# The MLP's first token block, made during the last chunk's convolution

## The chip, the core and the metric

One core of a Trainium2 chip runs the whole kernel. The metric is the device time of one execution in microseconds (us). TensorE (PE) does the matmuls, with the loading of its weights shown as PEld; VectorE (DVE), ScalarE (ACT) and GpSimd (POOL) work on elements; SyncE (SP) mainly issues DMA transfers. Each engine takes its instructions in the order of the compiled program, and waits where an operand or a buffer isn't there yet.

## The reference

One decoder layer on x of 2048 rows by 1024 columns, float32:

```python
h = rms_norm(x, attn_norm_g); z = h @ w_in          # q, k, v, gate_b, gate_c, xc
y_attn = swa_sink_attention(norm(q), norm(k), v, sinks)   # window 128, 8 heads of 64
y_conv = gate_b * short_conv(gate_c * xc, conv_w)         # 3 taps, 512 channels
x = x + concat(rms_norm(y_attn), rms_norm(y_conv)) @ w_out
x = x + square(relu(rms_norm(x) @ w_up)) @ w_down         # 4096 wide
```

## The kernel before, in words

**Mixer.** The rows are done in four chunks of 512 (`NCHUNK`, `NT` = 4 tiles of 128 rows each; the attention's tiles are called b0 to b15, so the last chunk has b12 to b15). Each fp32 matrix is split into a high and a low part, and a product is three matmuls (`mm3`, lines 267 to 269). For a tile, `qk_transpose` turns queries and keys (PE: L619, L621; ACT and DVE split them: L624, L625, L628, L629), `softmax` multiplies them (`psc`, L646) and works on the scores on ACT and DVE (L654 to L671), and `values` turns the probabilities (`ptp`, L682), splits and masks them (L688 on ACT, L689 on DVE, L695 on POOL), multiplies by v (`po`, L734) and finishes the tile on ACT and DVE (L742 to L750). The convolution of a chunk has two `conv_pair`s. Each has three groups of weights (wc, wx, wb), two output tiles for each group, 24 matmuls for a tile (`pc`, `px`, `pb`); DVE multiplies and adds the taps (L798 to L803, L815, L819). The output projection of a chunk has a half for the convolution (half 1, `pout3_1_*` in the last chunk) and one for the attention (half 0). Half 0 is left over to the next chunk, where it runs as `before`, ahead of the convolution.

**Order of the work.** `besides` is a generator with everything that runs beside the attention: `before`, then the two conv_pairs, then the projection's half 1. The attention's functions call `fill(n)` to step it, with the numbers of the table FILL. On top of that stands a scheduler: each instruction has a priority (`ahead(i)` raises it by `PRIO[chunk][i]`, which for `ahead(9)` in the last chunk is 0), and the scheduler decides each engine's order when the program is compiled. SP's transfers are one queue, in order. Weights come from DRAM by `weights` (L236, 1 MB each for the high and the low part) into two pairs of buffers of tag "w" and one of tag "raw", in turn: in the last chunk wc and wx in "w", wb in "raw", for both pairs, then the four pieces of the projection (`w_wo`).

**First block of the MLP.** The MLP multiplies 2x2 blocks by seven products instead of eight (`ORDER`). Its first token block is rows 0 to 1023, done by chunks 0 and 1. Each x operand is made from x1 in DRAM: `load_turned` (L308) loads four pieces of 128 KB for a quarter jj, `turned` transposes (L314) and scales (L315) on DVE, `x_put` (L319) stores it in `xop`, and `x_sums` (L325) makes the four differences. For each of the four jj there are blocks 1 and 2 (turned from the first 512 rows, `xm0`), block 3 and one unnamed (from the second 512 rows, `xm1`), and the sums 5, 6, 7 and 4.

`prepare_firsts` (L890) makes blocks 1 and 2 for all jj during the last chunk's convolution, a step at every seventh step of it (`FIRST_X`). `prepare_mlp` (L908) does the rest beside the projection's half 1, in the buffers of the tags "h0" and "h1"; it reads blocks 1 and 2 back from `xop`. Behind it come the residual's rows for chunk 3 (`x1_3`, L950, tag "x1", 4 buffers of 1024 columns) in the code's order ahead of the projection, and the loads of the last weights. The chunk before stores its rows by L880.

Of the kernel before, what the change touches and what calls it, by code (L numbers as in the profile page):

```python
# [7 lines left out]
F32 = mybir.dt.float32  # L8
# [4 lines left out]
ALU = mybir.AluOpType  # L13
# [3 lines left out]
P = 128  # L17
# [17 lines left out]
CH = 512  # L35
NT = CH // P
NCHUNK = S // CH
# [7 lines left out]
ORDER = (1, 2, 6, 5, 3, 7, 4)  # L45
# [4 lines left out]
BW = 512  # L50
NB = BW // P
# [18 lines left out]
CHP = CH + 32  # L70
STEPS = 3
TS = 32
FIRST_X = 7
REST = 7
LATER = 250

# [27 lines left out]
def hymba_layer(  # L104
# [19 lines left out]
    nc = tc.nc  # L124
# [11 lines left out]
    pool = mixers_ctx.enter_context(tc.tile_pool(name="work", bufs=1))  # L136
# [4 lines left out]
    x1_dram = dram.tile([S, D], F32, name="x1_dram")  # L141
# [3 lines left out]
    xop_dram = [  # L145
        [dram.tile([P, BLK], F32, name=f"xop{tb}_{i}") for i in range(len(ORDER))] for tb in range(NTB)
    ]
# [7 lines left out]
    def bank(tag, name):  # L155
        return psum.tile([P, 512], F32, tag=tag, name=name, bufs=BANKS[tag])

    def row(tag, name, bufs, dt=F32):

        return pool.tile([P, D], dt, tag=tag, name=name, bufs=bufs)  # L160
# [28 lines left out]
    def rsqrt(dst, ms):  # L189

        nc.gpsimd.tensor_scalar(ms, ms, EPS, None, op0=ALU.add)
        nc.gpsimd.tensor_tensor(dst, ms, mhalf[:, : ms.shape[1]], op=ALU.pow)
# [3 lines left out]
    def ahead(i):  # L196

        offset = PRIO[stage[0]][i]
        return tc.high_priority(offset=offset) if offset else nullcontext()
# [103 lines left out]
    def load_turned(xb, src, r0, jj):  # L303

        for pg in range(4):
            rows = src[r0 : r0 + BW].rearrange("(q i) (k c) -> i k q c", i=TS, k=2)
            c0 = jj * P + pg * TS
            nc.sync.dma_start(  # L308
                xb[pg * TS : (pg + 1) * TS].rearrange("p (k q c) -> p k q c", k=2, c=TS), rows[:, :, :, c0 : c0 + TS]
            )  # L310

    def turned(xb, k, dst, g, rs_row):

        nc.vector.transpose(dst, xb[:, k * BW : (k + 1) * BW])  # L314
        nc.vector.scalar_tensor_tensor(dst, dst, g, rs_row, op0=ALU.mult, op1=ALU.mult)  # L315

    def x_put(tb, jj, i, b):

        nc.sync.dma_start(xop_dram[tb][ORDER.index(i)][:, jj * BW : (jj + 1) * BW], b)  # L319

    def x_sums(tb, jj, b11, b21, b12, b22, t1):


        def sub(i, dst, a, b):
            nc.vector.tensor_tensor(dst, a, b, op=ALU.subtract)  # L325
            x_put(tb, jj, i, dst)

        x_put(tb, jj, 3, b22)
        sub(5, t1, b12, b11)
        sub(6, b11, b22, t1)  # L330
        sub(7, b12, b22, b12)
        sub(4, b21, b21, b11)
# [12 lines left out]
    def parts(pool_, tag, name):  # L345
        return [pool_.tile([P, KD, CH], F32R, tag=f"{tag}{s}", name=f"{tag}{s}_{name}", bufs=1) for s in range(2)]

    def prepare(src, r0, gb, dst, name):

        xs = []  # L350

        def fetch(t):
            xt = row("xt", f"xt_{name}_{t}", 2)
            nc.sync.dma_start(xt, src[r0 + t * P : r0 + (t + 1) * P, :])
            with ahead(8):
                norm(xt, gb, f"{name}_{t}")
                xs.append(xt)

        fetch(0)
        fetch(1)  # L360
        yield
        for t in range(NT):
            yield from transposed(xs[t], dst, t, f"{name}_{t}")
            if t + 2 < NT:
                fetch(t + 2)
# [55 lines left out]
    h = parts(pool, "h", "a0")  # L421
# [103 lines left out]
    with tc.tile_pool(name="mix_small", bufs=1) as mix_small, tc.tile_pool(name="mix", bufs=1) as mix:  # L525
# [359 lines left out]
                                    rs_out(c)  # L885
                    yield

        rows_x = []

        def prepare_firsts():  # L890

            rows = pool.tile([P, 2, BW], F32, tag="gb", name="rs_rows", bufs=1)
            rows_x.append(rows)
            for i in range(2):
                nc.sync.dma_start(rows[:, i], rs_dram[i].partition_broadcast(P))
            for jj in range(NB):
                xb = row("xt", f"xt_m0_{jj}", 2)
                load_turned(xb, x1_dram, 0, jj)
                yield
                bs = row("xt", f"xm0_{jj}", 2)  # L900
                for k in range(2):
                    b = bs[:, k * BW : (k + 1) * BW]
                    with ahead(9):
                        turned(xb, k, b, g_cols[:, NB * k + jj : NB * k + jj + 1], rows[:, 0])
                    x_put(0, jj, 1 + k, b)
                    yield

        def prepare_mlp():  # L908

            xs = [pool.tile([P, 8, CH], F32, tag=f"h{i}", name=f"xm{i}", bufs=1) for i in range(2)]  # L910
            rows = rows_x[0]
            xts = {}

            def fetch(jj):
                for k in range(2):
                    src = xop_dram[0][ORDER.index(1 + k)]
                    nc.sync.dma_start(xs[0][:, 2 * jj + k], src[:, jj * BW : (jj + 1) * BW])
                xts[jj] = row("xt", f"xt_m1_{jj}", 2)
                load_turned(xts[jj], x1_dram, BW, jj)

            fetch(0)
            fetch(1)
            yield
            for jj in range(NB):
                bs = [xs[0][:, 2 * jj + k] for k in range(2)] + [xs[1][:, 4 * (jj % 2) + k] for k in range(3)]
                with ahead(9):
                    for k in range(2):
                        turned(xts[jj], k, bs[2 + k], g_cols[:, NB * k + jj : NB * k + jj + 1], rows[:, 1])
                if jj + 2 < NB:
                    fetch(jj + 2)  # L930
                x_sums(0, jj, *bs)
                yield

        def besides(c, before, h, yt, rc, x1, h_next, z_next):

            yield from before
            ssc = mix.tile([P, CH], F32, tag="ssc", name=f"ssc{c}", bufs=1)
            firsts_x = prepare_firsts() if c + 1 == NCHUNK else iter(())
            for j in range(2):
                for i, _ in enumerate(conv_pair(c, h, j, yt, ssc)):  # L940
                    if i % FIRST_X == 0:
                        next(firsts_x, None)
                    yield
            for _ in firsts_x:
                pass
            x1 += [] if c else x0
            for t in range(NT if c else 0):
                r = (c * NT + t) * P
                xr = row("x1", f"x1_{c}_{t}", NT)
                nc.sync.dma_start(xr, xf[r : r + P, :])  # L950
                x1.append(xr)
            out = out_projection(c, 1, yt, rc, x1)
            if c + 1 < NCHUNK:
                h_next += parts(pool, "h", f"h{c + 1}")
                steps = prepare(xf, (c + 1) * CH, g_row[0], h_next, f"a{c + 1}")
            else:
                steps = prepare_mlp()
            for i, _ in enumerate(steps):
                yield
                for j in range(STEPS):  # L960
                    next(out, None)
                    yield
                    if (i, j) == PC:
                        pc = bank("tr", f"pc{c}")
                        for t in range(NT):
                            nc.tensor.matmul(
                                pc[:, t : t + 1], ssc[:, t * P : (t + 1) * P], mean, start=True, stop=True
                            )
                        ms = mix_small.tile([P, NT], F32, tag="msc", name=f"ms_c{c}", bufs=1)

                        with tc.high_priority(offset=SOON):
                            if c:
                                nc.vector.tensor_copy(ms, pc[:, :NT])
                                rsqrt(rc, ms)
                            else:
# [97 lines left out]
        g_cols = const.tile([P, KD], F32, name="g_cols")  # L1073
# [15 lines left out]
        for c in range(NCHUNK):  # L1089
            left, h, z = mixers(c, left, h, z)  # L1090
# [8 lines left out]
    pool = up_ctx.enter_context(tc.tile_pool(name="mlp_up", bufs=1, reuse_waits="tile"))  # L1099
# [247 lines left out]
    steps = [(p, g) for p in ORDER_DOWN for g in range(NCG // 2)]  # L1347
# [93 lines left out]
    pool = ctx.enter_context(tc.tile_pool(name="mlp_down", bufs=1, reuse_waits="tile"))  # L1441
# [131 lines left out]
```

## Time and profile before

| what | value |
|---|---|
| time, median of 3 runs | 1964.53 us (1963.91 to 1967.26) |
| the profiled execution | 1962.7 us |
| its span in the trace | 1961.0 us |
| mean granted clock of TensorE | 0.989 |
| PE busy | 1915.9 us (98%) |
| DVE, ACT, POOL busy | 1213.3, 827.3, 275.2 us |
| the attention's last left projection ends, the last chunk's convolution begins | 564 us |
| the projection's half 1 waits longest | 674.4 to 693.2 us |
| the MLP's first matmuls | about 730 us |

The page cuts the span into 40 slices of 49 us and gives the busy tenths of each engine in each. A table by stretch (the windows) gives the length of the stretch, then busy us and instruction counts of PE, PEld, DVE, ACT and POOL, the granted clock of TensorE (1.00 is full), the share of the DMA engines and GB/s. A group's row has: line, engine, operation, output and inputs, shape, count, then busy us and the mean of one in ns, then idle time before it and what ended it. A row of the waits has the engine and its line, who released it, us in total, how often, the longest.

### The profile page before, as it was taken

Reading aid. Unit: us, or ns where it says so; the run is one execution under the profiler, and the core shown is the slowest. Engines: PE = TensorE matmul, PEld = TensorE weight load, DVE = VectorE, ACT = ScalarE, POOL = GpSimd, SP = SyncE. Lnnn points to the kernel's source line nnn. Section 1 sums busy time; section 2 is a strip of 40 time slices with the busy share of each in tenths; the row PEclk is TensorE's granted clock in tenths of the full one; section 3 lists DMA queues with packets and bytes.
Section 4 is the critical chain, followed back from the end, with each engine's and each line's share of the span. In section 5 each row is a group of like instructions: output and inputs, shape, how many; then the busy total and the mean of one; then the engine's idle time right before and its main releaser. Section 6 shows DMA issues by size and latency. Waiting matters only on the chain.

```text
span 1961.0 us, 24748 instructions
## 1 busy us (share of the span) xinstructions
PE 1915.9 (98%) x8961; PEld 1595.4 (81%) x8961; DVE 1213.3 (62%) x1896; ACT 827.3 (42%) x1577; POOL 275.2 (14%) x475
## 2 busy tenths in 40 slices
PE   9999999999999689899999999999999999999999
PEld 9878877888888468788888888888888888888887
DVE  4885657447567838788878766666544334447541
ACT  6564444335344217355466555454332232222320
POOL 2122212312222201222201101011000000100000
PEclk9999999999999789999999999999999999999999
DMA  9774865574675778978775544437964457776641
GB/s 323 279 278 122 264 251 172 197 233 151 211 238 179 209 278 284 221 216 235 242 227 207 172 150 163 140 122 275 385 235 139 151 169 227 249 233 215 217 140 54
DMA packets 270540, 414.37 MB, mean 211 GB/s; under 512 B 85064, under 2 KB 174160, under 8 KB 258640
## 3 DMA queue, kind: packets, MB, share of 16 engines
q1 hardware_dynamic: 241664, 337.25, 52.7%
q0 software_dynamic: 15488, 51.40, 7.2%
q10 hardware_dynamic: 13264, 24.13, 3.3%
q8 instruction: 71, 1.16, 0.3%
q14 instruction: 53, 0.43, 0.1%
HBM read 286.87 MB, written 125.84 MB: 210 GB/s over the span
## 4 chain that ended last, share of the span: by engine, by line
PE 91%; DMA 3%; DVE 3%; ACT 1%; POOL 1%; issue 0%; SPq 0%; DVEq 0%; ACTq 0%
PE d L1533 31%; PE u L1426 30%; PE pout L268 3%; PE pout L267 3%; PE pout L269 3%; PE pz L267 2%; PE pz L268 2%; PE pz L269 2%; PE pc_c L269 2%; PE px_c L267 1%; PE px_c L269 1%; PE px_c L268 1%; PE pc_c L267 1%; PE pc_c L268 1%; PE psc_b L646 1%; PE po_b L734 1%
## 5 line engine op out<-in xcount | busy, mean ns | idle before, releaser
L1426 PE MATMUL u<-op_x,wop 128*128 128x512 f32 x2688 | 612.5, 390 | 5.4 <-DVE wop L398 5.4
L1533 PE MATMUL d<-op_w,op_f 128*128 128x512 f32 x2688 | 609.4, 389 | 0.0
L1426 PEld LDWEIGHTS u<-op_x,wop 128*128 128x128 f32 x2688 | 506.3, 188 | 111.5 <-DVE wop L398 5.8
L1533 PEld LDWEIGHTS d<-op_w,op_f 128*128 128x128 f32 x2688 | 504.7, 188 | 104.6
L382 DVE TENSOR_TENSOR op_f<-op_f 128x1024 fp32r<-128x1024 f32 x112 | 136.9, 1224 | 234.2 <-ACT op_f L381 233.9
L381 ACT CAST op_f<-op_f 128x1024 fp32r<-128x1024 f32 x112 | 117.6, 1051 | 355.2 <-DMA op_f<-fop 354.7
L397 ACT CAST wop<-wu 128x512 fp32r<-128x512 f32 x156 | 96.4, 620 | 92.4 <-PE u L1426 89.9
L398 DVE TENSOR_TENSOR wop<-wu,wop 128x512 fp32r<-128x512 f32 x156 | 110.1, 707 | 36.1 <-ACT wop L397 18.3
L1162 POOL DMA_DIRECT2D fop<-s x96 | 52.1, 543 | 447.9 <-DVE s L1165 443.5
L1168 DVE TENSOR_TENSOR u<-u,u 128x512 f32<-128x512 f32 x128 | 87.7, 685 | 22.9 <-PE u L1426 22.9
L382 DVE TENSOR_TENSOR op_w<-raw,op_w 128x1024 fp32r<-128x1024 f32 x56 | 68.3, 1221 | 25.0 <-ACT op_w L381 24.8
L381 ACT CAST op_w<-raw 128x1024 fp32r<-128x1024 f32 x56 | 58.8, 1052 | 43.2 <-PE d L1533 20.4
L267 PE MATMUL pout<-w_wo,yt_c 128*128 128x512 f32 x128 | 52.6, 417 | 18.8 <-DMA w_wo<-wo 18.8
L663 ACT ACTIVATE sc_b<-sc_b,ngm_b 128x128 f32<-128x128 f32 x128 | 49.6, 389 | 30.9 <-DVE ngm_b L660 30.9
L1174 ACT ACTIVATE u<-u 128x512 f32<-128x512 f32 x64 | 40.4, 632 | 47.7 <-DVE u L1168 45.7
L695 POOL TENSOR_SCALAR_AFFINE_SELECT pp_b<-pp_b 128x512 fp32r<-128x512 f32 x60 | 42.3, 715 | 117.0 <-ACT pp_b L688 59.0
L1375 POOL DMA_DIRECT2D wds<-raw x16 | 8.5, 534 | 332.5 <-DVE raw L1373 322.8
L381 ACT CAST op_x<-op_x 128x1024 fp32r<-128x1024 f32 x28 | 29.1, 1049 | 59.3 <-DMA op_x<-xop 59.0
L397 ACT CAST wop<-wu_s 128x512 fp32r<-128x512 f32 x64 | 39.4, 619 | 33.6 <-PE u L1426 29.6
L398 DVE TENSOR_TENSOR wop<-wu_s,wop 128x512 fp32r<-128x512 f32 x64 | 45.9, 718 | 11.6 <-ACT wop L397 11.4
L268 PE MATMUL pout<-w_wo,yt_c 128*128 128x512 f32 x128 | 51.8, 405 | 0.8 <-DMA w_wo<-wo 0.8
L269 PE MATMUL pout<-w_wo,yt_c 128*128 128x512 f32 x128 | 52.2, 408 | 0.0
(253 smaller groups left out, 3139.8 us busy)
## 6 DMA issues: line engine op xcount, KB each, us to landing
op_f<-fop SPq DMA_DIRECT2D x112, 512.0 KB, 4.3
raw<-in_w_down_dram SPq DMA_DIRECT2D x72, 512.0 KB, 4.3
wu<-in_w_up_dram SPq DMA_DIRECT2D x128, 256.0 KB, 3.9
w_wo<-wo SPq DMA_DIRECT2D x24, 1024.0 KB, 6.8
fop<-s POOLq DMA_DIRECT2D x96, 256.0 KB, 2.5
fop<-u ACTq DMA_DIRECT2D x64, 256.0 KB, 2.7
op_x<-xop SPq DMA_DIRECT2D x28, 512.0 KB, 7.4
w_q<-qkv SPq DMA_DIRECT2D x24, 512.0 KB, 6.0
```

Of the source, the lines that this page charges most:

```text
L267: nc.tensor.matmul(ps, st(0), mv(0), start=first, stop=False)
L268: nc.tensor.matmul(ps, st(0), mv(1), start=False, stop=False)
L269: nc.tensor.matmul(ps, st(1), mv(0), start=False, stop=last)
L381: nc.scalar.copy(op[:, 0], raw)
L382: nc.vector.tensor_tensor(op[:, 1], raw, op[:, 0].bitcast(F32), op=ALU.subtract)
L397: splits.append(nc.scalar.copy(hi, blk).ins)
L398: nc.vector.tensor_tensor(lo, blk, hi.bitcast(F32), op=ALU.subtract)
L663: nc.scalar.activation(sc[:, hd, :], sc[:, hd, :], AF.Exp, bias=ngm[:, hd : hd + 1], accum_out=den[:, hd : hd + 1])
L1162: eng.dma_start(fop_dram[tb][ORDER_DOWN.index(i)][n // 2][:, n % 2], b)
L1168: return nc.vector.tensor_tensor(dst, ps, b, op=ALU.add).ins
L1426: nc.tensor.matmul(pt, wops[i][:, a, k, :], xops[tb, p][k // 2][:, b, k % 2, :], start=p not in GOES_ON and k + j == 0, stop=k + j == NB + ...
L1533: nc.tensor.matmul(ps[tb][j], fs[tb][:, a, k, j * P : (j + 1) * P], w[:, b, k, :], start=first and p not in GOES_ON and k + n == 0, stop=l ...
```

## The change

`prepare_firsts` goes, and `prepare_mlp` does both parts. It starts in `before` (a step at every fourth, `FIRST_X`), and goes on in the conv_pairs (a step at every fourth, `SECOND_X`). The second half uses the rows of tag "xt" for the turned blocks and rows of tag "x1", the residual's, for the blocks read back and the sums. The puts are collected and issued a step later (`put_late`). What isn't done when the convolution ends is issued right there, ahead of the residual's rows. Beside the projection there are now eight empty steps where there were five with work. New lines of the changed kernel: the differences are L940, the turned loads are called at L924; lines behind the change have moved by about 22.

```diff
-FIRST_X = 7
+FIRST_X, SECOND_X = 4, 4
...
-        def prepare_firsts():
+        def prepare_mlp():
...
+            def put(jj, i, b):
+                late.append((jj, i, b))
+
+            def put_late():
+                for jj, i, b in late:
+                    x_put(0, jj, i, b)
+                late.clear()
+
+            def fetch(i, jj):
+                xb = row("xt", f"xt_m{i}_{jj}", 2)
+                load_turned(xb, x1_dram, i * BW, jj)
+                return xb
+
             for jj in range(NB):
-                xb = row("xt", f"xt_m0_{jj}", 2)
-                load_turned(xb, x1_dram, 0, jj)
+                xb = fetch(0, jj)
                 yield
-                bs = row("xt", f"xm0_{jj}", 2)
+                bs = halves(row("xt", f"xm0_{jj}", 2))
                 for k in range(2):
-                    b = bs[:, k * BW : (k + 1) * BW]
                     with ahead(9):
-                        turned(xb, k, b, g_cols[:, NB * k + jj : NB * k + jj + 1], rows[:, 0])
-                    x_put(0, jj, 1 + k, b)
-                    yield
-
-        def prepare_mlp():
-
-            xs = [pool.tile([P, 8, CH], F32, tag=f"h{i}", name=f"xm{i}", bufs=1) for i in range(2)]
...
+                        turned(xb, k, bs[k], gain(k, jj), rows[:, 0])
+                    put(jj, 1 + k, bs[k])
+                yield
+                put_late()
             for jj in range(NB):
-                bs = [xs[0][:, 2 * jj + k] for k in range(2)] + [xs[1][:, 4 * (jj % 2) + k] for k in range(3)]
+                xb = fetch(1, jj)
+                b11, b21 = halves(row("x1", f"xm1_{jj}", NT))
+                for i, b in ((1, b11), (2, b21)):
+                    nc.sync.dma_start(b, xop_dram[0][ORDER.index(i)][:, jj * BW : (jj + 1) * BW])
+                put_late()
+                yield
+                b12, b22 = halves(row("xt", f"xm0_{jj}", 2))
+                t5, t6 = halves(row("x1", f"xm2_{jj}", NT))
                 with ahead(9):
-                    for k in range(2):
-                        turned(xts[jj], k, bs[2 + k], g_cols[:, NB * k + jj : NB * k + jj + 1], rows[:, 1])
-                if jj + 2 < NB:
-                    fetch(jj + 2)
-                x_sums(0, jj, *bs)
+                    turned(xb, 0, b12, gain(0, jj), rows[:, 1])
+                put_late()
                 yield
+                with ahead(9):
+                    turned(xb, 1, b22, gain(1, jj), rows[:, 1])
+                put(jj, 3, b22)
+                yield
+
+                def sub(i, dst, a, b):
+                    with ahead(9):
+                        nc.vector.tensor_tensor(dst, a, b, op=ALU.subtract)
+                    put(jj, i, dst)
+
+                put_late()
+                sub(5, t5, b12, b11)
+                sub(6, t6, b22, t5)
+                yield
+                put_late()
+                sub(7, b12, b22, b12)
+                sub(4, b21, b21, t6)
+                yield
+            put_late()
...
-            yield from before
+            turning = prepare_mlp() if c + 1 == NCHUNK else iter(())
+            for i, _ in enumerate(before):
+                if i % FIRST_X == 0:
+                    next(turning, None)
+                yield
             ssc = mix.tile([P, CH], F32, tag="ssc", name=f"ssc{c}", bufs=1)
-            firsts_x = prepare_firsts() if c + 1 == NCHUNK else iter(())
             for j in range(2):
                 for i, _ in enumerate(conv_pair(c, h, j, yt, ssc)):
-                    if i % FIRST_X == 0:
-                        next(firsts_x, None)
+                    if i % SECOND_X == 0:
+                        next(turning, None)
                     yield
-            for _ in firsts_x:
+            for _ in turning:
                 pass
...
-                steps = prepare_mlp()
+                steps = range(2 * NT)
```

More of the change, by code (lines that the diff above doesn't have):

```diff
@@ L886, in out_projection @@
                     yield
-        rows_x = []
-        def prepare_firsts():
+        def prepare_mlp():
             rows = pool.tile([P, 2, BW], F32, tag="gb", name="rs_rows", bufs=1)
-            rows_x.append(rows)
             for i in range(2):
                 nc.sync.dma_start(rows[:, i], rs_dram[i].partition_broadcast(P))
+            halves = lambda xt: [xt[:, k * BW : (k + 1) * BW] for k in range(2)]
+            gain = lambda k, jj: g_cols[:, NB * k + jj : NB * k + jj + 1]
+            late = []
+            def put(jj, i, b):
[8 more added lines that the diff above has]
+                return xb
@@ L908, in prepare_mlp @@
-        def prepare_mlp():
-            xs = [pool.tile([P, 8, CH], F32, tag=f"h{i}", name=f"xm{i}", bufs=1) for i in range(2)]
-            rows = rows_x[0]
-            xts = {}
-            def fetch(jj):
-                for k in range(2):
[L916 to L923, printed above, removed]
-            for jj in range(NB):
-                bs = [xs[0][:, 2 * jj + k] for k in range(2)] + [xs[1][:, 4 * (jj % 2) + k] for k in range(3)]
-                with ahead(9):
-                    for k in range(2):
-                        turned(xts[jj], k, bs[2 + k], g_cols[:, NB * k + jj : NB * k + jj + 1], rows[:, 1])
-                if jj + 2 < NB:
-                    fetch(jj + 2)
-                x_sums(0, jj, *bs)
-                yield
```

## The prediction

> **What bounds the kernel now.** I read the page first. The span is 1961.0 us, and TensorE (PE) is busy for 98% of it, so only a stretch in which PE stands or runs at half clock can give time back, and a new such stretch costs its whole length.
>
> ```profile
> span 1961.0 us, 24748 instructions
> PE   9999999999999689899999999999999999999999
> ...
> PEclk9999999999999789999999999999999999999999
> ```
>
> Each slice is 49 us. The dips are in slices 14 and 15 (637 to 735 us): the end of the last chunk's convolution and its output projection, where the change works. Next I cut that place into stretches; the first column after the window is its length, then busy time of PE, weight loads, DVE, ACT and POOL, then the granted clock and the DMA share.
>
> ```profile
> 564.00:645.00 81.00, 81.00 (x403) 67.97 (x402) 56.93 (x130) 40.04 (x134) 12.76 (x24) 1.00 0.64 181
> 645.00:649.00 4.00, 2.19 (x13) 1.33 (x11) 4.00 (x8) 1.87 (x4) 1.74 (x3) 1.00 0.65 154
> 649.00:659.20 10.20, 7.02 (x24) 5.58 (x25) 7.88 (x15) 3.56 (x9) 5.83 (x7) 0.50 0.95 301
> 659.20:674.40 15.20, 14.13 (x60) 10.36 (x58) 12.38 (x24) 4.00 (x7) 2.53 (x5) 1.00 0.93 208
> 674.40:676.30 1.90, 0.01 (x1) 0.00 (x0) 1.86 (x4) 0.00 (x0) 0.79 (x2) 1.00 1.07 381
> 676.30:693.20 16.90, 0.00 (x0) 0.03 (x1) 9.54 (x15) 0.00 (x0) 0.00 (x0) 0.50 0.85 289
> 693.20:700.20 7.00, 6.21 (x14) 4.45 (x15) 0.00 (x0) 0.00 (x0) 0.00 (x0) 0.50 1.00 421
> ```
>
> The convolution up to 645 us has no hole at all: 81.00 of 81.00 us. From 645 to 700.2 us PE misses 1.81 + 3.18 + 1.07 + 1.89 + 16.90 + 0.79 = 25.6 us. The waits say for what, and the chain of waits says why that came late:
>
> ```profile
> PE pout L267 <- DMA w_wo<-wo: 18.8, 1, 18.8
> PE po_b L734 <- DVE pp_b L689: 4.9, 3, 2.8
> ```
> ```profile
> 684.19 1.91 DVE xm L325 x3
> 686.12 0.32 SPq L319
> 686.49 0.45 SPq L236
> 686.99 8.57 DMA w_wo<-wo
> ```
>
> The 18.8 us are one wait for the weights of the second half of the convolution's projection. Their load (L236) stands on SP's queue behind the x_put transfers (L319), and the last of these waits for DVE's sums (L325). The weights are late because SP is in order, not because DMA is short.
>
> **What the change removes.** Transposes, scalings, sums and puts all go ahead of the residual's row loads and of the projection's weights; in the compiled order of the changed kernel no put stands on SP before the projection's loads any more. So the 18.8 us go. What is late next is the weight load itself: its pair of buffers comes free at the convolution's last matmul, and the first projection half (48 matmuls and b15's value products, over 11 us) covers a landing of 8.57 us. I cost it at nothing; without the cover it is 8.57 us. The 4.9 us for pp_b leave this place too, but come back below, since the chains of b14 and b15 stay. Half clock goes with the holes: 7.02 and 6.21 us of work at clock 0.50 would take half, 3.5 and 3.1 us less. Removed: 25.6 + 6.6 = **32.2 us**.
>
> **What it adds.** The work itself is small: 8 transposes, 8 scalings and 16 sums of one block are pulled into the convolution, some 23 us of DVE by the rows below, where DVE is busy 56.93 of 81.00 us. That much would fit. What counts is the order. Before, the compiled order lays score, transpose and value products of the attention one by one between convolution matmuls; in the changed kernel they stand in bunches (16 psc_b12, 16 psc_b13, then 44 matmuls of pc_c without a break, then ptp_b12, po_b12, 16 psc_b14, ptp_b13, po_b13, then 44 of px_c, and so on). In a bunch PE has nothing else to run while ACT, DVE and POOL make its operands, and in DVE's order the new transposes and sums now stand ahead of just these operands. SP also has each low half of a weight pair behind stores, turned loads and puts. The durations (count, busy us, mean ns):
>
> ```profile
> L646 PE MATMUL psc_b<-kw,qt_b 128*128 128x256 f32 x64 | 16.4, 282 | 0.0
> L315 DVE SCALAR_TENSOR_TENSOR xm<-xm,g_cols,rs_rows 128x512 f32<-128x512 f32 x12 | 9.0, 757 | 0.1
> L314 DVE STREAM_TRANSPOSE xm<-xt_m 128x512 f32<-128x512 f32 x12 | 8.2, 698 | 0.4 <-PE pb_c L268 0.4
> L325 DVE TENSOR_TENSOR xm<-xm 128x512 f32<-128x512 f32 x12 | 7.6, 685 | 0.1
> L803 DVE SCALAR_TENSOR_TENSOR y_c<-u_c,cw,y_c 128x512 f32<-128x512 f32 x8 | 6.2, 779 | 0.1
> L743 DVE TENSOR_TENSOR o_b<-po_b,o_b 64x512 f32<-64x512 f32 x8 | 5.5, 684 | 0.4 <-ACT o_b L742 0.4
> L689 DVE TENSOR_TENSOR pp_b<-ptp_b,pp_b 128x512 fp32r<-128x512 f32 x8 | 5.3, 677 | 2.7 <-ACT pp_b L688 2.6
> L688 ACT CAST pp_b<-ptp_b 128x512 fp32r<-128x512 f32 x8 | 4.4, 588 | 8.5 <-PE ptp_b L682 8.5
> L625 DVE TENSOR_TENSOR qt_b<-ptq_b,qt_b 64x512 fp32r<-64x512 f32 x6 | 4.1, 688 | 1.8 <-ACT qt_b L624 1.7
> L325 DVE TENSOR_TENSOR xm<-xm,xm 128x512 f32<-128x512 f32 x4 | 3.2, 796 | 0.1
> L798 DVE TENSOR_TENSOR u_c<-px_c,u_c 128x512 f32<-128x512 f32 x4 | 2.7, 686 | 4.3 <-PE px_c L269 4.3
> L801 DVE TENSOR_SCALAR y_c<-u_c,cw 128x512 f32<-128x512 f32 x4 | 1.9, 486 | 0.5 <-POOL halo L799 0.5
> L747 DVE TENSOR_TENSOR at_b<-o_b,at_b 128x512 fp32r<-128x512 f32 x4 | 2.7, 684 | 0.0
> L629 DVE TENSOR_TENSOR kw<-ptk_b,kw 64x128 fp32r<-64x128 f32 x6 | 1.7, 289 | 0.1
> L628 DVE TENSOR_TENSOR kw<-ptk_b,kw 64x128 fp32r<-64x128 f32 x6 | 1.7, 282 | 1.3 <-ACT kw L627 1.2
> L749 DVE TENSOR_TENSOR o_b<-o_b 128x256 f32<-128x256 f32 x4 | 1.7, 421 | 0.8 <-ACT o_b L748 0.7
> L750 DVE TENSOR_TENSOR o_b<-o_b 128x128 f32<-128x128 f32 x4 | 1.1, 287 | 0.1
> ```
> ```profile
> w_wc<-wc SPq DMA_DIRECT2D x4, 1024.0 KB, 7.7
> ```
> ```profile
> 541.94 0.80 SPq L236 DMA_DIRECT2D w_wc<-wc  x2
> ...
> 565.01 0.32 SPq L880 DMA_DIRECT2D x_dram<-x  x1
> ```
>
> I lay the changed orders on a time axis with these rows; the stalls, in order:
> 1. *First weights.* Both halves of w_wc were issued at 541.94 us. The low half now stands behind the store of chunk 2's last rows (565.01), so it lands at about 565.4 + 7.7 = 573. PE's work ahead of its first use (32 psc_b of some 0.12 us each when they follow one another, a few others) lasts from 564.0 to about 569.5; the bunch psc_b13 also waits for DVE's qt_b13 behind a transpose. 3 to 6 us, I take 4.3.
> 2. *After pc_c.* psc_b14 needs the second half of qt_b14. On DVE stand ahead of it: two L689, one L625, b14's keys (L628, L629) and a small copy of values, together about 1 us, two L314, two L315, and then L625 itself: 1.35 + 0.69 + 1 + 1.40 + 1.51 + 0.69 = 6.6, and about 2.6 us for the first transpose, cast and hand-overs: 9.2. PE has 3.2 us of po_b12 and transposes beside it: 6.0. Then ptp_b13 to po_b13 is the kind of chain that cost 1.8 and 3.2 us above (645 to 659): 2.3. Together 8.3, between 3 (if the first L625s run early) and 10.5.
> 3. *After px_c.* psc_b15 needs the second half of qt_b15. After the last px_c matmul DVE has L798 0.69, L801 0.49, two L803 1.56, two L743 1.37, first L625 and L747 1.37, b15's keys (L628, L629) and b12's squares (L749, L750) 0.28 + 0.29 + 0.42 + 0.29 = 1.28, two L314 1.40, two L315 1.51, four sums (three at 0.685, one at 0.796) 2.85, and L625 0.69: 13.2 us. PE has 1.4 us of transposes and pb_c beside it: 11.8, between 8 and 14. This is the largest term, and no other matmul may pass it.
> 4. *After pb_c*, the rest of psc_b15, then ptp_b14 and po_b14: the chain of item 2's end twice, 4.6, between 2 and 7.
> 5. *Later weights* behind the puts of the third and fourth block: 1.5, between 0 and 4.
>
> Idle time added: 4.3 + 8.3 + 11.8 + 4.6 + 1.5 = 30.5 us, between 16 and 41.5. The clock comes on top. In the rows above the granted clock went to 0.50 at 649.0 after the 1.81 us of holes from 645 on. A later stall shows what the return costs:
>
> ```profile
> 804.00:809.40 5.40, 5.40 (x13) 4.24 (x14) 5.39 (x10) 2.67 (x6) 1.62 (x3) 0.50 1.06 324
> 809.40:820.00 10.60, 10.60 (x48) 8.76 (x48) 10.56 (x18) 4.80 (x9) 0.54 (x1) 1.00 0.92 268
> ```
>
> 13 matmuls at 0.415 us instead of 0.221 are 2.5 us; the stretch from 649 cost 3.5. With one drop for each of items 1 to 4 at 2.7 that is 11 us, between 2.5 (item 3 alone) and 17.5 (one more, at 3.5 each).
>
> The Trainium skill speaks of this ("TensorE: Matmul & The Clock Gate", "HAM oscillation — how this bites in real kernels"): the clock falls when PE idles for more than some 3.4 us at a stretch. The row of 645 to 649, where the clock fell after less idle than that, does not bear it out literally. By the page items 1 and 4, which come in pieces, would keep the clock, and my sum would be about 5 us lower; I go by the rows.
>
> **Sum.** -32.2 + 30.5 + 11 = +9.3 us. The profiled execution took 1962.7 us (its span and 1.7 us around it), so 1972.0 by it; the median of the runs is 1.8 us above it, so **1973.8 us**. Everything behind 730 us stays.
>
> **Rivals.**
> - *The new waits are mostly covered* (the other side, faster). DVE has room (56.93 of 81.00), and if it is ahead of PE when a bunch begins, items 2 and 3 shrink, because the turned blocks are then done before the attention asks. It decides at item 3: if the four sums are over before px_c ends, its 13.2 us fall by 5.8. With items of 2, 4, 6, 3 and 0 and two clock drops it is 15 + 5.4 = 20.4, so -11.8: 1952.7 us. For it: the removed wait is certain and in one piece. Against it: DVE's order places L798, which needs the end of px_c, ahead of L314 and the sums.
> - *About the same.* Added 28 to 36 us against 32.2: 1960.5 to 1968.5 us.
> - *Weights late all through.* SP is in order, every weight pair from w_wx on stands behind puts that wait for DVE, as L236 stood behind L319 at 686 us; DMA shares reach 0.95 there. If each of the four later pairs comes 3 us later than laid out, 12 us more: 1986 us. For it: the chain of waits above is this very mechanism. Against it: between 564 and 645 the share is only 0.64.
>
> **How the numbers follow.** Forecast 0.50, covered 0.20, the same 0.12, weights late 0.18. So faster by over 0.2% (3.9 us, about what a measurement here can tell from no change) 0.20, within it 0.12, slower 0.68. The range goes from 1953, where the covered case lies, to 1986, the late weights; for the slower cases alone it is 1969 to 1986.
>
> **What would show it.** Right: no wait of pout L267 for w_wo near 18.8 us; PE idle at psc_b L646 behind DVE's qt_b L625, about 6 us after pc_c and 12 after px_c; a wait of pc_c L269 for w_wc before 575 us; clock 0.50 in several stretches between 565 and 650; the first matmul of the MLP (u) about 9 us later. Wrong: a convolution as gapless as the 81.00 of before, or the holes without clock drops, or pout still waiting for w_wo.

## The result and the profile after

The changed kernel takes 1980.09 us (median of 4 runs, 1975.39 to 1982.17) beside 1965.39 us for the kernel before in the same comparison: a ratio of 1.0071, 95% interval 1.005 to 1.0092. It is slower, by 14.7 us where 9.3 were forecast, and inside the range of 1953 to 1986. The profiled execution took 1979.13 us, so the traces stand 16.4 us apart (1979.13 and 1962.7).

The page of the changed kernel cuts its span into 40 slices of some 49 us. PE's dip has moved from slices 14 and 15 to slices 12 to 14, and the clock row has it in 12 and 13:

```profile
span 1977.4 us, 24753 instructions
...
PE   9999999999987899999999999999999999999999
...
PEclk9999999999987999999999999999999999999999
```

The stretches of the last chunk in the changed kernel (length, then busy us of PE, PEld, DVE, ACT, POOL, granted clock, DMA share):

```profile
566.10:576.50 10.40, 7.83 (x42) 6.34 (x40) 8.22 (x20) 5.40 (x16) 2.28 (x6) 0.84 1.02 180
576.50:581.10 4.60, 0.02 (x1) 0.02 (x1) 4.14 (x17) 4.14 (x21) 0.00 (x0) 0.87 0.26 8
581.10:598.80 17.70, 17.25 (x65) 12.97 (x65) 5.63 (x11) 6.95 (x26) 2.51 (x4) 0.84 0.60 135
598.80:624.20 25.40, 20.44 (x80) 16.41 (x80) 18.16 (x42) 7.90 (x32) 3.61 (x7) 0.80 0.47 128
624.20:634.20 10.00, 1.15 (x6) 0.65 (x6) 9.73 (x18) 4.15 (x10) 0.37 (x2) 0.67 0.96 324
634.20:667.20 33.00, 30.05 (x130) 23.48 (x130) 17.73 (x40) 9.44 (x32) 3.88 (x7) 0.94 0.68 192
667.20:672.90 5.70, 0.05 (x1) 0.00 (x0) 2.64 (x5) 1.75 (x3) 0.00 (x0) 0.93 1.00 364
672.90:698.20 25.30, 24.82 (x99) 19.88 (x99) 14.75 (x25) 4.90 (x8) 0.43 (x2) 0.88 0.85 325
698.20:747.90 49.70, 48.52 (x223) 39.72 (x222) 24.43 (x37) 11.10 (x16) 8.89 (x15) 1.00 0.64 232
```

The last row is the projection: 1.2 us missing of 49.7, at full clock. What stood there before is gone. The convolution ahead of it, gapless before, now lacks 31.7 - 1.2 = 30.5 us. The waits of PE between 564 and 748 us say for what:

```profile
PE px_c L267 <- DMA w_wx<-wx: 5.7, 1, 5.7
PE pa_b L755 <- DVE o_b L750: 5.5, 1, 5.5
PE pc_c L269 <- DMA w_wc<-wc: 4.6, 1, 4.6
PE psc_b L646 <- DVE qt_b L625: 4.0, 2, 3.1
PE po_b L734 <- DVE pp_b L689: 2.9, 2, 1.7
PE ptq_b L619 <- DVE o_b L743: 2.7, 1, 2.7
PE psc_b L646 <- DVE kw L628: 1.5, 1, 1.5
```

Two of them are loads of weights (10.7 us, with a third of 0.4); the others are the attention's steps waiting for DVE with nothing beside them. SP, which loads the weights, waits itself, and so do all loads behind it. Its longest wait in the changed kernel (564 to 700 us), and then the same line in the kernel before (564 to 660 us); in the changed kernel L308 has the turned loads, and L924 reads blocks 1 and 2 back:

```profile
SPq L319 <- DVE xm L315: 42.9, 7, 15.2
```
```profile
SPq L319 <- DVE xm L315: 16.8, 4, 13.1
```

### The profile page after: what moved, and what is told of

Its sections match the earlier page's. It is cut to its first block, busy times and chain, and to the rows that moved or that the text cites. A ratio compares the mean times of both kernels' runs of the same rounds, so it can differ in the third digit from the quotient of the medians.

```text
span 1977.4 us, 24753 instructions
## 1 busy us (share of the span) xinstructions
PE 1926.1 (97%) x8961; PEld 1601.4 (81%) x8961; DVE 1209.8 (61%) x1896; ACT 827.5 (42%) x1577; POOL 273.3 (14%) x475
## 4 chain that ended last, share of the span: by engine, by line
PE 90%; DMA 4%; DVE 3%; ACT 2%; POOL 1%; issue 1%; SPq 0%; DVEq 0%; ACTq 0%; POOLq 0%
PE d L1555 31%; PE u L1448 30%; PE pout L268 2%; PE pout L269 2%; PE pout L267 2%; PE pz L267 2%; PE pz L268 2%; PE pz L269 2%; PE px_c L269 2%; PE px_c L267 2%; PE px_c L268 1%; PE pc_c L269 1%; DMA w_wc<-wc 1%; PE pc_c L268 1%; PE pc_c L267 1%; PE psc_b L646 1%
## 5 line engine op out<-in xcount | busy, mean ns | idle before, releaser
L398 DVE TENSOR_TENSOR wop<-wu,wop 128x512 fp32r<-128x512 f32 x156 | 110.0, 706 | 35.8 <-ACT wop L397 18.1
L382 DVE TENSOR_TENSOR op_w<-raw,op_w 128x1024 fp32r<-128x1024 f32 x56 | 68.3, 1221 | 25.3 <-ACT op_w L381 25.2
L267 PE MATMUL pout<-w_wo,at_b 128*128 128x512 f32 x128 | 50.3, 393 | 0.0
```

Source lines behind the costliest of these rows:

```text
L267: nc.tensor.matmul(ps, st(0), mv(0), start=first, stop=False)
L382: nc.vector.tensor_tensor(op[:, 1], raw, op[:, 0].bitcast(F32), op=ALU.subtract)
L398: nc.vector.tensor_tensor(lo, blk, hi.bitcast(F32), op=ALU.subtract)
```

## The experiments

Ratios are to the kernel before in the same comparison, with 95% intervals. Where an edit adds lines, those behind it have moved by one or a few.

**e1: weights far ahead.**

```diff
-            for d, t in zip(parts_dram[name], hl):
-                nc.sync.dma_start(t.bitcast(F32), d)
+            with tc.high_priority(offset=1000) if c + 1 == NCHUNK else nullcontext():
+                for d, t in zip(parts_dram[name], hl):
+                    nc.sync.dma_start(t.bitcast(F32), d)
```

> The changed kernel with the last chunk's weight loads at a priority of 1000 above the rest, nothing else edited; in the compiled order the attention then stands between the convolution's matmuls again, one by one. Theory (the added 32 us of idle PE and the clock drops come from weights late on SP's queue and from the bunched order that follows from it): the convolution has less than 6 us of idle PE, no clock 0.50 from 564 to 640, and the time falls to about 1950 us, 30 below the changed kernel, if the puts that now stand behind waiting weights are still in time for the MLP. Rival (the 23 us of DVE work pulled into the convolution stall PE by themselves, whatever the order of the loads): still 25 us or more of idle PE, 1972 to 1982 us.

Measured: 1979.14 us, ratio 1.0075 (1.0058 to 1.0092). The convolution and then the hole behind it, in the stretches of e1, and PE's longest wait:

```profile
569.60:650.10 80.50, 80.38 (x398) 67.36 (x396) 56.27 (x127) 40.15 (x133) 11.29 (x24) 1.00 0.65 208
...
676.20:708.90 32.70, 0.00 (x0) 0.00 (x0) 16.11 (x26) 0.00 (x0) 0.80 (x2) 0.50 0.71 199
```
```profile
PE pout L268 <- DVE x L874: 32.7, 1, 32.7
```

Half of the theory holds: with the weights in time and the attention unbunched, the stalls in the convolution vanish. The time doesn't follow; it lies where the rival had it, though not by its mechanism. DVE is busy for 56.27 us there, no more than in the kernel before, since a part of the turning has slipped behind the convolution; so this run doesn't yet decide on DVE's work (e6 does for a part of it, the sums). Now the turning waits on SP behind weights that wait for their buffers, ends late, and holds the x1 rows into which the residual of chunk 3 must be loaded; the projection's products can't be added up, and PE stops for 32.7 us.

**e2: weights some way ahead**, as e1 with an offset of 300.

> As the run before it, with a priority of 300: weights up to the first group of the second conv_pair stand ahead of the puts, the later ones among them; the compiled order is unbunched up to px of the second pair and bunched from there. Theory: the stalls up to pb of the first pair go (about 20 of the 32 us and two to three clock drops), a few of the later ones stay, 1952 to 1962 us. Rival (DVE's work): 1972 to 1982 us.

Measured: 1979.9 us, 1.0077 (1.0062 to 1.0093). The same balance: 7.8 us of PE missing in the convolution, and 27.1 us of pout waiting for the residual. The forecast of 1952 to 1962 missed for the reason of e1; the rival's time fits, its cause doesn't.

**e3: turning behind the attention on DVE.**

```diff
-    (200, 20, 180, -10, 0, 0, 40, 40, -20, 0, 0, 30),
+    (200, 20, 180, -10, 0, 0, 40, 40, -20, -100, 0, 30),
```

> The changed kernel with the turned blocks and sums 100 lower in priority on DVE; the bunched order of PE stays, the loads stay, but the third and fourth block's transposes and sums now stand behind qt_b15 on DVE instead of ahead of its second half. Theory: the term of 8.9 us idle after px (waits for DVE's o_b and qt_b) shrinks by about 5.7 us, the weight waits (4.6 for w_wc, 5.7 for w_wx) stay, 1972 to 1977 us. Rival (DVE's work alone): with the attention first on DVE most of the idle goes, 1955 to 1965 us.

Measured: 1990.51 us, 1.0143 (1.012 to 1.0165): slower still, outside both forecasts. PE's longest waits, and SP's longest (564 to 700 us):

```profile
PE px_c L269 <- DMA w_wx<-wx: 8.7, 2, 8.3
PE px_c L267 <- DMA w_wx<-wx: 5.8, 1, 5.8
```
```profile
SPq L319 <- DVE xm L315: 66.7, 8, 17.9
```

The later DVE scales a block, the longer SP stands at its put (66.7 us instead of 42.9) and the later the weights behind it are issued. DVE's order reaches PE by way of SP.

**e4: the kernel before, with the weights ahead** (the edit of e1).

> The kernel before, with the same priority of 1000 for the last chunk's weight loads: the projection's weights no longer stand behind the puts. Theory (the 18.8 us were only SP's order): the wait of pout L267 for w_wo falls below 3 us and the time by 15 to 25 us, to about 1945 us. Rival (the sums, now later, hold up the MLP's first products instead): the wait comes back at the first u, 1958 to 1966 us.

Measured: 1951.28 us, 0.9937 (0.9922 to 0.9953), faster than both kernels. The 18.8 us of pout are gone altogether. PE's waits from 560 to 800 us:

```profile
PE u L1427 <- ACT wop L398: 20.7, 1, 20.7
PE u L1427 <- DVE wop L399: 2.3, 1, 2.3
```

Both predictions of the run hold in part, and the time lies between them: the wait came back at the first u, but u still starts 11.3 us earlier (718.57 instead of 729.86).

**e5: the first half early, alone.** In the kernel before, `prepare_firsts` is stepped in `before` (`FIRST_X = 4`), the rest unchanged.

```diff
-FIRST_X = 7
+FIRST_X = 4
...
-            yield from before
+            firsts_x = prepare_firsts() if c + 1 == NCHUNK else iter(())
+            for i, _ in enumerate(before):
+                if i % FIRST_X == 0:
+                    next(firsts_x, None)
+                yield
...
-            firsts_x = prepare_firsts() if c + 1 == NCHUNK else iter(())
```

> The kernel before with one part of the change alone: blocks 1 and 2 are started in the left projection (a step at every fourth) instead of in the convolution; the second half and the sums stay beside the projection, in h0 and h1. In its compiled order the attention is bunched up to psc_b14 and stands one by one from there, and on SP the turned loads and puts of the third and fourth quarter stand ahead of low halves of w_wc and w_wx. Theory (weights behind turned loads and puts, and the bunching from that): the stalls at the first weights and after pc come as in the changed kernel (10 to 12 us of idle PE before 612 us, two or three clock drops), the wait of 18.8 us stays, 1974 to 1982 us. Rival (the second half and its sums make the stalls): no idle before 640 us, 1963 to 1967 us.

Measured: 1971.08 us, 1.0033 (1.0021 to 1.0045), between the two forecasts: 2.4 us missing ahead of 612 us instead of 10 to 12, though at two of the forecast places (psc_b behind kw L628 and qt_b L625) and with two clock drops. The wait for w_wc stayed out. The wait for w_wo shrank to 13.9 us, and 5.4 us appeared at pa_b. So this half alone makes a part of the loss (6.1 of some 15 us), not most of it.

**e6: no sums.** Blocks 5, 6, 7 and 4 are put unsubtracted.

```diff
-                    with ahead(9):
-                        nc.vector.tensor_tensor(dst, a, b, op=ALU.subtract)
-                    put(jj, i, dst)
+                    put(jj, i, a)
```

> The changed kernel without its 16 sums (blocks 5, 6, 7 and 4 are put without being subtracted, so 11.4 us of DVE are left out); SP's order is the same and PE's nearly. Theory (order and late weights): the wait at pa_b12 and qt_b15 loses the four sums' 2.85 us, the puts and the weights behind them come up to 3 us earlier a quarter, 1971 to 1977 us. Rival (DVE's added work stalls PE): half of the added DVE work gone takes half of the added idle with it, 1958 to 1966 us.

Measured: 1981.36 us, 1.0083 (1.0063 to 1.0104). 11.4 us of DVE fewer, and no gain; the rival falls for the sums, and so does my own 3 to 9 us. On DVE in the changed kernel, then in e6, the squares of b12 (L750) and the second half of qt_b15 (L625):

```profile
633.75 0.28 DVE L750 TENSOR_TENSOR o_b<-o_b 128x128 f32<-128x128 f32 x1
...
635.87 0.69 DVE L625 TENSOR_TENSOR qt_b<-ptq_b,qt_b 64x512 fp32r<-64x512 f32 x1
```
```profile
633.37 0.69 DVE L625 TENSOR_TENSOR qt_b<-ptq_b,qt_b 64x512 fp32r<-64x512 f32 x1
634.09 0.29 DVE L750 TENSOR_TENSOR o_b<-o_b 128x128 f32<-128x128 f32 x1
```

qt_b15 comes 2.5 us earlier, as the sums' 2.85 us had it. But in the changed kernel PE stood at pa_b12 first, which waits for L750; it went on with pa_b12 and four pb at 634.2 us and took up psc_b15 at 636.7. In e6 it goes on with psc_b15 at 634.2, the same time. So the sums don't bind there. Ahead of L749 stand the two transposes and scalings in both runs (630.3 to 632.9 us in the changed kernel); that they are what binds was not tried by leaving them out.

**e7: puts on POOL.**

```diff
-        nc.sync.dma_start(xop_dram[tb][ORDER.index(i)][:, jj * BW : (jj + 1) * BW], b)
+        eng = nc.gpsimd if not tb else nc.sync
+        eng.dma_start(xop_dram[tb][ORDER.index(i)][:, jj * BW : (jj + 1) * BW], b)
```

> The changed kernel with the first block's puts issued by POOL instead of SP. The low half of w_wc now stands behind the fourth quarter's turned loads, which wait for a row buffer that the puts set free; PE's order is as bunched as before. Theory (what counts is that weights stand behind anything that waits for DVE or a buffer): the weight waits stay or grow, 1976 to 1986 us. Rival (the puts alone are what the weights wait for): the weights' waits of 4.6 and 5.7 us go, 1964 to 1970 us.

Measured: 1971.72 us, 1.0031 (1.0016 to 1.0047), between the two forecasts. PE's two longest waits, and the one for weights that is left:

```profile
PE ptp_b L683 <- DVE sc_b L658: 7.6, 2, 3.8
PE ptp_b L683 <- issue: 5.4, 1, 5.4
...
PE pc_c L269 <- DMA w_wc<-wc: 0.7, 1, 0.7
```

The waits for weights shrink from 10.7 us to 0.7, so the puts were what held the weights, against my theory of anything on the queue. PE still lacks 24.7 us in the convolution, 5.8 less than in the changed kernel. The longest waits are now at ptp_b, 7.6 us for DVE's part of the softmax (L658) and one of 5.4 for which the profile names no engine; the compiled order is as bunched as before. So most of the idle time stays without the late weights. How much of it is the bunched order and how much DVE's added work, which is all in the convolution here too, this run doesn't part.

**e8: the kernel before, first loads of the MLP ahead as well.** As e4, with the two first x operands and the four first weight pieces at 1000.

```diff
...
+            with tc.high_priority(offset=1000) if early and name[:2] == "x0" else nullcontext():
                 nc.sync.dma_start(flat(raw), flat(src))
...
+        with tc.high_priority(offset=1000) if n < 4 and i == 1 else nullcontext():
             nc.sync.dma_start(pieces(b), ...)
```

> The kernel before with the last chunk's weights at a priority of 1000 as in e4, and with the loads of the MLP's first two x operands and of its first four weight pieces ahead as well, which stood behind 15 puts there. Theory (the 20.7 us before the first u in e4 were SP's order once more; the first eight products need blocks 1 and 2 alone and last 96 matmuls, 21.8 us): u starts right behind the projection, and product 6 finds its operands, 1928 to 1936 us. Rival (the sums end too late for product 6 or the weights of product 2 wait for their buffers): the wait comes back among the first u, 1942 to 1952 us.

Measured: 1958.96 us, 0.9975 (0.9963 to 0.9986): faster than before, slower than e4. u starts right behind the projection, at 696.5 us, does 48 matmuls and waits 14.6 us for the weights of product 2, whose loads stand behind the puts too, and later 3.1 us. The rival's place, at a worse time than it gave. It loses to e4 by 7.7 us in the medians and by 4.4 in the traces (1955.41 us, the fastest of its ten runs, and 1950.99), with nearly as much idle time; some 3 of the 4.4 us are half clock, since 14.8 us of PE's work behind the first u stand at 0.50 where e4 has 8.5. The rest of the 7.7 is open.

**e9 and e12: the small store later.** POOL's store of 512 row norms is made to depend on a gate product of the first conv_pair (that of its second tile, `ct == 1`). e9 does it on POOL with a new buffer of four columns, e12 on DVE in place; e12's edit:

```diff
-                                if t + 1 == NT:
+                                if t + 1 == NT and c + 2 < NCHUNK:
                                     rs_out(c)
...
+                    if c + 1 == NCHUNK and ct == 1:
+                        r4 = rs_x1[:, (c - 1) * NT : c * NT]
+                        nc.vector.scalar_tensor_tensor(r4, y[:, :NT], 0.0, r4, op0=ALU.mult, op1=ALU.add)
+                        rs_out(c - 1)
```

> The changed kernel with one DMA moved: POOL's store of 512 single floats (2 KB, the row norms of chunk 2, 12.8 us from issue to landing, issued at 569.4 us) now depends on a zero made from the convolution's gate product and so starts about 640 us; PE's order is unchanged. In the changed kernel the low half of w_wc, issued at 567.4, took 13.7 us where 7.7 is usual, and in the kernel before three kinds of transfer in flight beside this store took 14 to 15 us. Theory (the small store holds up what is in flight): w_wc lands in 8 to 9 us, the wait of 4.6 us at pc goes, with one clock drop, 1973 to 1977 us, and transfers near 645 us are slow instead. Rival (w_wc is slow for another reason, as its place behind 1.5 MB of stores): the wait stays, 1978 to 1982 us.

Measured, e9: 1992.49 us, 1.0147 (1.0132 to 1.0162). The wait for w_wc was gone and yet the time was outside both forecasts: the matmuls of the MLP ran slower. Hence the run without the new buffer:

> As e9, the small store behind the first gate product, but without e9's new buffer: DVE adds zero times the gate product to the row norms in place, so no other buffer moves. In e9 the wait of 4.6 us at pc was gone and the first u 4.3 us earlier counted from pc, while all 2688 matmuls of u and of d ran slower (busy 625.4 and 613.8 us against 611.8 and 609.4 in the changed kernel), which made the whole time 12 us worse. Theory (the store holds up w_wc, and e9's loss comes from the new buffer, which moves all that lie behind it): u and d back at 611 to 613 and 609.4 us, no wait for w_wc, 1973 to 1978 us. Rival (e9's loss comes from the later store itself): u and d slow again, 1988 to 1994 us.

Measured, e12: 1975.35 us, 1.0063 (1.0049 to 1.0077). The transfers from 567 to 582 us in the changed kernel (KB each, median us to landing), then in e12 from 565 us:

```profile
w_wc<-wc SPq DMA_DIRECT2D x1, 1024.0 KB, 13.7
...
rs_dram<-rs_x POOLq DMA_DIRECT2D x1, 2.0 KB, 12.8
```
```profile
w_wc<-wc SPq DMA_DIRECT2D x1, 1024.0 KB, 5.4
```

The wait of 4.6 us at pc is gone, and from the first pc to the first u it is 175.3 us instead of 181.9. The transfers near 645 us are not slow instead, as e9's forecast had it: the second pair's w_wc take 8.9 us there (8.3 in the changed kernel), and SP issues nothing from 635.8 to 649.7 us, while the moved store (641.8 us) takes 9.6. The time, as forecast, is 4.7 us below the changed kernel's median, at the lower edge of its runs, and the intervals of the two overlap; the waits are what tells them apart. The MLP's matmuls in e9, then in e12:

```profile
L1454 PE MATMUL u<-op_x,wop 128*128 128x512 f32 x2688 | 625.4, 395 | 3.5 <-DVE wop L398 3.5
L1561 PE MATMUL d<-op_w,op_f 128*128 128x512 f32 x2688 | 613.8, 391 | 0.0
```
```profile
L1452 PE MATMUL u<-op_x,wop 128*128 128x512 f32 x2688 | 611.9, 390 | 5.4 <-DVE wop L398 5.2
L1559 PE MATMUL d<-op_w,op_f 128*128 128x512 f32 x2688 | 609.4, 389 | 0.0
```

**e10: e1 with the residual's rows elsewhere.** Chunk 3's rows go to the h0 buffer, free behind the convolution, at a priority of 1000.

```diff
...
+                    if not t:
+                        xh = pool.tile([P, 8, CH], F32, tag="h0", name="x1_h", bufs=1)
+                    xr = xh[:, 2 * t : 2 * t + 2].rearrange("p a c -> p (a c)")
+                    with tc.high_priority(offset=1000):
+                        nc.sync.dma_start(xr, xf[r : r + P, :])
```

> As e1 (the changed kernel with weights at 1000), with the residual's rows of chunk 3 in the convolution's free h0 buffer instead of the x1 rows that the turning holds, and loaded ahead too. Theory (the 32.7 us in e1 were only the rows' buffers): pout no longer waits for the residual, the idle time falls from 41 us behind the convolution to under 15, 1940 to 1955 us. Rival (the sums end too late whatever buffers there are, and the MLP's first operands stand behind them): the wait moves to the first u, 1965 to 1980 us.

Measured: 1969.96 us, 1.0027 (1.0016 to 1.0037). The 32.7 us at pout are gone, so they were the rows' buffers. The wait moves to u again, 19.7 us in six pieces, and the time is the rival's:

```profile
PE u L1456 <- ACT wop L398: 19.7, 6, 11.8
```

**e11: all ahead.** e10 with the edit of e8 and `EARLY = 8`, the four further pieces in z rows.

> As e10, with the loads of the MLP's first two x operands and of its first eight weight pieces ahead of the puts as well (four of the pieces in the attention's z rows). Theory (each stall found so far was a load behind something on SP): the convolution, the projection and the first 96 matmuls of u have no stall over 5 us; the sums end near 700 us, before product 6 needs them, 1925 to 1938 us. Rival (the sums or their reload are late for product 6): one wait of 10 to 20 us there, 1942 to 1955 us.

Measured: 1974.17 us, 1.0053 (1.0038 to 1.0068). From 569.7 to 725 us PE lacks only 1.5 us. One u stands among the projection's products at 682.3 us; the others start behind the projection at 701.8, 28.0 us ahead of the kernel before. Then:

```profile
PE u L1461 <- DMA wu<-in_w_up_dram: 28.2, 1, 28.2
```

On SP the last puts end at 740.3 us there and the next weights stand behind them. Both forecasts fail: the place is the rival's, the size is beyond it.

## Why the prediction was right, and where not

**What is removed** held as predicted: no wait of pout for w_wo, the projection at full clock with 1.2 us missing, 25.6 us idle and 6.6 us of half clock gone.

**What is added** held in kind and in sum, not in the single terms; that the sum of the idle time came out within 1.2 us is luck, since errors of some 8 us in both directions cancel. The terms of the working beside the gaps of the trace (from the waits above and the smaller ones of the same view):

| term | predicted idle us | measured |
|---|---|---|
| 1 first weights, psc_b13 | 4.3 | 4.6 + 1.5 + 0.9 = 7.0 |
| 2 after pc | 8.3 | 3.1 + 1.1 + 0.8 = 5.0 |
| 3 after px | 11.8 | 2.7 + 0.7 + 5.5 = 8.9 |
| 4 after pb | 4.6 | 1.7 + 0.6 + 0.4 = 2.7 |
| 5 later weights | 1.5 | 5.7 + 0.4 = 6.1 |
| in the projection | 0 | 1.2 |
| sum, with smaller gaps | 30.5 | 31.7 |
| clock | 11 | 27.2 us busy at 0.50, half of it 13.6 |

Term 1 was too small, since the load of w_wc took 13.7 us and not the 7.7 of its group; e12 shows the small store beside it as the cause. Term 5 was the worst, and like term 1 outside its own bounds: it was given 1.5 with no row behind it, but the second pair's w_wx was late because SP stood at the puts (15.2 of the 42.9 us right ahead of it), which was the third rival's mechanism, at one pair instead of four. e3 (more of it) and e7 (without it) show that. Terms 2 to 4 were too large by 8.1 us together, because PE had more work beside the chains than was laid out. In term 2 the chain ended some 8 us after pc (593.8 to 601.8) instead of 9.2, and PE had 4.6 us of work beside it instead of 3.2.

**One reading of term 3 falls.** The chain of 13.2 us on DVE was right to a microsecond (px ends at 624.2, the second half of qt_b15 at 636.6). But PE didn't wait for its end: the sign that the forecast named, PE idle at psc_b behind qt_b after px, isn't there. The 8.9 us stand at ptq_b and ptk_b behind o_b (L743) and at pa_b12 behind L750, and from 634.2 us on PE had four pb to do, although the forecast let no other matmul pass the waiting psc_b15. The four sums bought nothing when they were left out (e6). The rival "covered" took them as its point of decision; that was wrong as well.

**Three small slips of the working.** Puts do still stand on SP ahead of the projection's loads (the last at 675.9 us, w_wo from 687.0), and the residual's rows wait 7.2 us for one of them, though PE doesn't feel it. Only the first two pairs of weights have their halves apart on SP; from the first w_wb on both stand together behind puts. By its own figures the rival "about the same" runs from 1960.3 to 1968.3, 0.2 us lower than written.

**The balance.** From the first pc to the first u it is 181.9 us instead of 165.6, so 16.3 longer. Idle time accounts for 6.1 of it (31.7 - 25.6) and half clock for 7.0 (13.6 - 6.6). The remaining 3.2 us lie where no gap is shown. The row of the psc_b doesn't show them, though their mean rose from 282 to 362 ns: 31 of the 64 start at half clock, which is counted already, and their busy time fell from 16.4 to 13.7 us.

```profile
L646 PE MATMUL psc_b<-kw,qt_b 128*128 128x256 f32 x64 | 13.7, 362 | 6.4 <-DVE qt_b L625 4.0 <-DVE kw L628 1.5 <-DVE sc_b L657 0.8
```

Counted in both traces from each start to the next, without the gaps and with half clock taken off, the attention's own products (psc_b, ptp_b, po_b, ptq_b, ptk_b) take some 4 us more than before (25.2 instead of 21.3) and the others a little less; this is an estimate from the timelines, and no run tried it.

So the stretch is 7.0 us longer than the +9.3 of the forecast: 1.2 of idle time, 2.6 of clock and these 3.2, which the forecast didn't have. The first u comes 18.1 us later than before, where about 9 was named: 16.3 us in the stretch, and the first pc is 1.8 us later as well. The MLP behind it is 1.7 us shorter. The medians stand 14.7 us apart, a little less than the two traces.

**The clock.** The forecast had four drops, one for each of items 1 to 4. There were six up to the projection: two each in items 1 and 2 (at 573.1 and 579.9, at 600.4 and 610.6), one in item 3 (627.7), none in item 4 and one at the late weights (672.1). Half clock followed short gaps at some of them. PE in the changed kernel about 573 us, the idle time before each group in brackets:

```profile
571.31 0.76 PE L646 MATMUL psc_b<-kw,qt_b 128*128 128x256 f32 x2 [1.48 <-DVE kw L628]
572.97 3.48 PE L646 MATMUL psc_b<-kw,qt_b 128*128 128x256 f32 x14 [0.90 <-DVE qt_b L625]
```

The clock was at 0.50 from 573.1 to 576.5 us (0.84 as a mean of the first stretch above), before the long wait of 4.6 us began, and again at 610.6 after gaps of 0.5 and 1.1. But after gaps of 0.6, 0.4 and 1.7 us between 648 and 654 it stayed at 1.00, so the runs give no length of a gap that decides. The Trainium skill ("TensorE: Matmul & The Clock Gate", "HAM oscillation — how this bites in real kernels") puts the limit at gaps of some 3.4 us; by its reading these drops would be missing, and the trace has them, so the rows decide here.

**Where the gain went.** The runs show two causes in the changed kernel. One is SP's order: weights stand behind puts that wait for DVE. Without that the waits for weights fall by 10.0 us and the idle time by 5.8 (e7); with more of it the time grows (e3). The other is the bunched attention with the turning on DVE beside it, which leaves 24.7 us of idle time without late weights (e7); e6 takes the sums out of it as a cause, while the transposes and scalings were not tried alone. Behind both stands that the preparation of the block is a chain of load, transpose and put on SP and DVE, which has to go somewhere. If it goes ahead of the weights, the convolution has these waits (the changed kernel). If the weights go ahead, the projection waits for the rows it holds (e1, e2), and if it gets other rows, the MLP waits for what stands behind its puts (e10, e11). Why the compiled order bunches the attention was not measured on the chip by itself; it was bunched where the weights stood behind puts or turned loads (in e2 and e5 in part), and unbunched in e1, e4, e8, e10 and e11, where they stood ahead.

## What to carry to other kernels

When work is moved into a gapless stretch, look first at what its DMAs stand ahead of on an in-order queue, and what each of them waits for; the free share of the engine that does the work says little (in e6 11.4 us less of DVE's work gained nothing). Here a wait for a load that stands behind others was better cured by moving that load (e4, 0.9937) than by moving the work in front of it. Then follow the chain on: with the weights ahead, each cure made the next load in line the late one, and none of the further reorderings beat the first.

## What the runs showed of the hardware that was not expected

- A store of 512 single floats (2 KB) took 12.5 and 12.8 us, and transfers beside it were slow: 1 MB of w_wc needed 13.7 us beside it and 5.4 and 5.7 without it (e12, e9), turned loads and puts issued 5 to 7 us after it 8.1 and 9.0 us beside it and 3.8 and 3.0 without it (e12). In the kernel before, w_wb, the turned loads and a put took 14.8, 14.1 and 14.7 us beside it, where PE had no gap.
- A new buffer of four columns went with 13.6 us more for u and 4.4 us more for d (e9 beside the changed kernel); without it both were back (e12). In the timelines the u of e9 start evenly every 232 ns instead of 227, so it is no stall. e12 also does on DVE what e9 did on POOL, and that moved addresses do it was not tried by itself.
